# Softmax division behind the product with the values, its reciprocals carried to rows through DRAM

## Chip, core and metric

One core of one Trainium2 chip runs the whole program in one launch. The metric is the device time of that launch in microseconds (us); lower is better. All data are float32; products run on TensorE as fp32r splits (a high and a low part).

## What is computed

A stack of four attention layers (kinds MLA, SWA, FOX, MLA) on a 512 x 1024 sequence, then a second block with four token mixers (two of them attention), a gated feed-forward part and a gated embedding. What the change touches is the softmax that every attention head ends with, here of the dense layers:

```python
def one_block(n):
    s = jnp.einsum('bqhd,bkhd->bhqk', q_blk, k, preferred_element_type=jnp.float32) * scale
    ...
    s = jnp.where(k_pos[None, :] <= q_pos[:, None], s, NEG_INF)
    p = jax.nn.softmax(s, axis=-1).astype(v.dtype)
    return jnp.einsum('bhqk,bkhd->bqhd', p, v)
...
return (o * jax.nn.silu(gate)) @ w_out
```

SWA adds the exponential of a sink to the sum. There are 16 heads in each of the four layers, taken in 8 pairs, and 8 heads (4 pairs) in the mixers: 72 heads, 36 pairs.

## The kernel before

The engines' order is not written by hand. The program is traced in Python, and a scheduler reorders the instructions of each engine by its own estimate of when each could run; each engine, and SP's queue of transfers, then works through its list strictly in that order. So an edit can move instructions that it does not touch.

`pairs` runs a layer's heads. For each pair it prepares the next pair (`prep`: projections of queries and keys on TensorE, splits on ACT and DVE, and in MLA small SBUF moves through SP, L477), then runs `attend` for both heads, joins their outputs into one tile `og` (L462, L463; 64 rows a head, queries along the free axis), computes the gate `u` (`gate`, L606) and multiplies in `gated` (L468 to L470), on POOL for every pair but the layer's last, where DVE does it. The result is split into the high and low operands of the output projection.

`attend` does one head. TensorE makes the scores of four query blocks into PSUM tiles `ps_s`; DVE adds the mask or bias and takes the row maximum (L403); a few 128x4 instructions make the exponent's bias (L409 to L415); ACT takes four exponentials in place in tile `p` and sums each row (L419). Then DVE takes one reciprocal of the four sums (L422) and the four blocks of `p` are scaled by it: on DVE in the layers (L427, four instructions a head), in the mixers two on ACT (L429), one on DVE and one on POOL (L431). TensorE transposes the scaled blocks into `ps_t` (L443), ACT and DVE split them into `pth` and `ptl` (L184, L185), and TensorE multiplies them with the values into the one PSUM tile `ps_o` (L452), which the join empties. PSUM tiles: three `ps_acc`, two `ps_s`, two `ps_t`, one `ps_o`.

```python
nc.vector.reciprocal(st[:, 3], st[:, 2])
for i in range(T):
    a = sc[:, off[i]:off[i] + w[i]]
    how = ("vvvv" if "cq" in s.phase_tags else "aavp")[i]
    if how == "v":
        nc.vector.tensor_scalar_mul(a, a, st[:, 3, i:i + 1])
```

Weights stream in through SP (L135, L146) into six tiles `wr`; ACT rounds each to `wh` (L138) and POOL subtracts for `wl` (L139), which frees `wr` again. In `mixers`, `rel_head` calls `attend` and the joined `og` is split without a gate. FOX has one trip through DRAM already: its forget values are stored (L719, tile `forget`) and read back, one row spread over 128 partitions (L256, tile `rope`).

Of the kernel before, what the change touches and what calls it, by code (L numbers as in the profile page):

```python
# [9 lines left out]
F32 = mybir.dt.float32  # L10
# [11 lines left out]
BUFS = dict(x=4, act=8, wr=6, wh=6, wl=6, st=6)  # L22
# [66 lines left out]
class Kern:  # L89
# [300 lines left out]
    def attend(s, s_mm, k0s, bias, scale, v, sink=None, shift=None):  # L390


        nc = s.nc
# [86 lines left out]
    def mla(s, j, li, xT, g_next):  # L480
# [63 lines left out]
        def head(d, p, e):  # L544
# [7 lines left out]
            return s.attend(s_mm, [0] * T, s.causal, scale, s.vsel(v, e))  # L552
# [33 lines left out]
    def pairs(s, order, prep, head, Wg, g0, xT, oT):  # L586

        order = list(order)
        u = {order[0]: s.gate(order[0], Wg, g0, xT)}
        d = prep(order[0])  # L590
        for p, after in zip(order, order[1:] + [None]):
            og = s.t("f", [P, S], name="og")
            nd = prep(after) if after is not None else None
            for e in range(2):
                s.join(og, e, head(d, p, e))
            if p not in u:
                u[p] = s.gate(p, Wg, g0, xT)
            s.gated(p, og, u[p], oT, after is None)
            d = nd
# [46 lines left out]
    def swa(s, j, li, xT, g_next):  # L646
# [24 lines left out]
        def head(d, p, e):  # L671
            hd = 2 * p + e
            q, (kd, kl), win = d
            return s.attend(lambda out, i, k0: s.qk_mm(out, i, k0, q, e, kd, kl), [0, 0, 1, 2],
                            lambda i: win[:, e, 128:] if i == 0 else win[:, e], 0.125, s.vsel(vt[p // 4], (p % 4) // 2),
                            sink=sinks[:, hd:hd + 1])
# [5 lines left out]
    def fox(s, j, li, xT, g_next):  # L682
# [61 lines left out]
        def head(d, p, e):  # L744
            q, (k, kl), v, bs = d
            return s.attend(lambda out, i, k0: s.qk_mm(out, i, k0, q, e, k[:, e], kl[:, e]), [0] * T,
                            lambda i: bs[e][i], 0.125, s.vsel(v, e), shift=cq[:, :, 2 * p + e])
# [195 lines left out]
    def rel_head(s, qk, v, h, e, og, sel=None):  # L943
# [12 lines left out]
        s.join(og, e, s.attend(lambda out, i, k0: s.qk_mm(out, i, k0, q, e, k[:, e], kl[:, e]), [0] * T, bias, 0.125, s.vsel(v, e)))  # L956

    def mixers(s, hT):
        W = s.I["w_in_2"][0]
# [3 lines left out]
        def heads(d, v, pr, h0, m, sel=None):  # L963
            og = s.t("f", [P, S], name="og")
            for e in range(2):
                s.rel_head(d, v[pr], h0 + 2 * pr + e, e, og, sel)
            s.split(og, mix.h(m + pr), mix.l(m + pr))
# [27 lines left out]
        heads(d1, vd, 1, 0, 4, s.sel)  # L995
# [141 lines left out]
```

## Time and profile before

| what | value |
|---|---|
| median of 3 runs | 1758.17 us (1758.05 to 1764.92) |
| the profiled execution's own time | 1762.84 us |
| its span, first to last instruction | 1761.1 us |
| TensorE (PE) busy | 1684.8 us, 96% |
| PE weight loads (PEld) busy | 1435.2 us, 81% |
| VectorE (DVE) busy | 962.0 us, 55% |
| ScalarE (ACT) busy | 873.8 us, 50% |
| GpSimd (POOL) busy | 854.4 us, 49% |
| TensorE's mean granted clock | 0.979 |

Busy shares are of the span of one profiled execution. A matmul's end is modelled and successive matmuls overlap, so a busy PE is not yet a PE at its peak. "Granted clock" is the share of TensorE's full speed that it was allowed in a stretch: 1.0 is 2.4 GHz, 0.5 is 1.2 GHz. The profile also tells, for each instruction that its engine stood idle for, which instruction released it.

### The profile page before, as it was taken

The page shows a single profiled execution, that of the slowest core. Times are in us where ns is not written, and L with a number is a line of the kernel's source. Part 1 is how long each engine was busy: PE and PEld are TensorE (multiplying, and loading weights), DVE is VectorE, ACT ScalarE, POOL GpSimd, SP SyncE. Part 2 cuts the span into 40 slices and gives each one's busy share as a digit, 9 for nine tenths or more (in the row PEclk, how much of TensorE's full clock was granted, in tenths as well). Part 3 has the DMA queues.
Part 4 walks back from the last instruction along what each step waited for, and adds up shares of the span by engine and source line. Part 5 has one row for each costly group of instructions (what it writes and reads, how often), then busy time and mean ns, then how long its engine had stood idle before and what let it go on. Part 6 is the DMA issues. An engine that isn't in the chain of part 4 may idle for free.

```text
span 1761.1 us, 25691 instructions
## 1 busy us (share of the span) xinstructions
PE 1684.8 (96%) x8818; PEld 1435.2 (81%) x8818; DVE 962.0 (55%) x2223; ACT 873.8 (50%) x2054; POOL 854.4 (49%) x775
## 2 busy tenths in 40 slices
PE   8999999999999999999999998999999999999999
PEld 7888878887788888778888877877778888888877
DVE  4587654677654665766587665599544222210053
ACT  4576543666445655633576642755544333332351
POOL 1644534444255665616644523745644444443571
PEclk9999999999999999999999998999999999999999
DMA  5434534322032333314444523332332333332332
GB/s 169 132 98 114 165 104 124 99 70 87 26 97 81 101 88 93 116 51 127 120 110 103 176 61 74 91 81 64 114 90 83 98 96 96 96 100 80 105 99 72
DMA packets 190339, 173.91 MB, mean 99 GB/s; under 512 B 14280, under 2 KB 154952, under 8 KB 190208
## 3 DMA queue, kind: packets, MB, share of 16 engines
q1 hardware_dynamic: 190208, 172.27, 33.9%
q8 instruction: 70, 1.15, 0.3%
q14 instruction: 61, 0.50, 0.1%
HBM read 150.94 MB, written 6.87 MB: 90 GB/s over the span
## 4 chain that ended last, share of the span: by engine, by line
PE 52%; DVE 9%; ACT 2%; issue 2%; POOL 2%; DMA 1%; SPq 0%; ACTq 0%; POOLq 0%; DVEq 0%
PE ps_acc L157 11%; PE ps_acc L158 11%; PE ps_acc L159 11%; PE ps_s L158 4%; PE ps_s L157 4%; PE ps_s L159 4%; PE ps_o L452 2%; PE ps_t L443 2%; DVE p L427 1%; DVE sel L926 1%; ACT p L419 1%; DVE m L925 1%; DVE p L403 1%; PE ps_s L238 1%; DVE ptl L185 1%
## 5 line engine op out<-in xcount | busy, mean ns | idle before, releaser
L139 POOL TENSOR_TENSOR wl<-wr,wh 128x512 fp32r<-128x512 f32 (+2 forms) x362 | 472.7, 1316 | 421.5 <-ACT wh L138 408.7
L138 ACT CAST wh<-wr 128x512 fp32r<-128x512 f32 (+2 forms) x368 | 223.6, 613 | 364.9 <-PE ps_acc L158 125.1
L157 PE MATMUL ps_acc<-act,wh 128*128 128x512 f32 (+1 forms) x880 | 331.5, 377 | 0.9 <-DVE v L620 0.8
L158 PE MATMUL ps_acc<-act,wh 128*128 128x512 f32 (+1 forms) x880 | 330.2, 375 | 0.3 <-DVE act L185 0.2
L159 PE MATMUL ps_acc<-act,wl 128*128 128x512 f32 (+1 forms) x880 | 330.1, 375 | 0.0
L157 PEld LDWEIGHTS ps_acc<-act,wh 128*128 128x128 f32 x880 | 165.6, 188 | 27.9 <-PE ps_acc L159 1.2
L159 PEld LDWEIGHTS ps_acc<-act,wl 128*128 128x128 f32 x880 | 165.3, 188 | 27.5
L158 PEld LDWEIGHTS ps_acc<-act,wh 128*128 128x128 f32 x880 | 165.4, 188 | 27.0 <-DVE act L185 0.7
L419 ACT ACTIVATE p<-p,st 128x256 f32<-128x256 f32 (+3 forms) x288 | 153.5, 537 | 32.8 <-DVE st L410 17.3
L157 PE MATMUL ps_acc<-wh,act 128*128 128x256 f32 (+3 forms) x384 | 134.5, 350 | 7.7 <-ACT act L469 3.1
L185 DVE TENSOR_TENSOR ptl<-ps_t,pth 128x512 fp32r<-128x512 f32 (+1 forms) x200 | 117.6, 597 | 38.5 <-ACT pth L184 37.7
L184 ACT CAST pth<-ps_t 128x512 fp32r<-128x512 f32 (+1 forms) x200 | 100.3, 516 | 72.5 <-PE ps_t L443 63.0
L443 PE MATMUL ps_t<-c_ident,p 128*128 128x128 f32 x672 | 116.9, 283 | 17.3 <-DVE p L427 12.4
L427 DVE TENSOR_SCALAR p<-p,st 128x256 f32<-128x256 f32 (+3 forms) x264 | 132.1, 559 | 1.8
L159 PE MATMUL ps_acc<-wh,act 128*128 128x256 f32 (+3 forms) x384 | 130.7, 341 | 0.1
L158 PE MATMUL ps_acc<-wl,act 128*128 128x256 f32 (+3 forms) x384 | 130.4, 340 | 0.0
L443 PEld LDWEIGHTS ps_t<-c_ident,p 128*128 128x128 f32 x672 | 82.0, 143 | 33.7 <-DVE p L427 13.2
L452 PE MATMUL ps_o<-pth,v 128*128 128x256 f32 (+3 forms) x288 | 90.1, 318 | 6.3 <-DVE og L463 4.4
L452 PE MATMUL ps_o<-ptl,v 128*128 128x256 f32 (+3 forms) x288 | 88.2, 335 | 4.3 <-DVE ptl L185 4.2
L157 PEld LDWEIGHTS ps_acc<-wh,act 128*128 128x128 f32 x384 | 77.8, 203 | 16.0 <-ACT act L469 3.3
L158 PEld LDWEIGHTS ps_acc<-wl,act 128*128 128x128 f32 x384 | 77.7, 202 | 5.1 <-issue 0.5
L159 PEld LDWEIGHTS ps_acc<-wh,act 128*128 128x128 f32 x384 | 77.1, 201 | 5.5 <-DVE act L185 0.3
(371 smaller groups left out, 3801.3 us busy)
## 6 DMA issues: line engine op xcount, KB each, us to landing
wr<-in_w_gate_up_dram SPq DMA_DIRECT2D x88, 256.0 KB, 2.8
wr<-in_fox_w_in_dram SPq DMA_DIRECT2D x60, 256.0 KB, 3.1
wr<-in_w_in_dram SPq DMA_DIRECT2D x48, 256.0 KB, 2.9
wr<-in_w_down_dram SPq DMA_DIRECT2D x44, 256.0 KB, 2.6
wr<-in_swa_w_in_dram SPq DMA_DIRECT2D x40, 256.0 KB, 2.9
wr<-in_mla_w_in_dram SPq DMA_DIRECT2D x32, 256.0 KB, 3.1
qk<-qk SPq DMA_DIRECT2D x32, 256.0 KB, 3.1
wr<-in_mla_w_out_dram SPq DMA_DIRECT2D x32, 256.0 KB, 3.5
```

The source lines that it names most:

```text
L138: nc.scalar.copy(h, raw)
L139: (nc.vector if dve else nc.gpsimd).tensor_sub(l, raw, h.bitcast(F32))
L157: mm(out, lh, rh, start=first, stop=False)
L158: mm(out, lh, rl, start=False, stop=False)
L159: return mm(out, ll, rh, start=False, stop=last)
L184: s.nc.scalar.copy(hi, src)
L185: s.nc.vector.tensor_sub(lo, src, hi.bitcast(F32))
L238: mm(out, q[:, e, c], kd[:, kk], start=True, stop=False)
L419: nc.scalar.activation(a, a, AF.Exp, bias=st[:, 1, i:i + 1], scale=scale, accum_out=st[:, 2, i:i + 1])
L427: nc.vector.tensor_scalar_mul(a, a, st[:, 3, i:i + 1])
L443: nc.tensor.transpose(ps[:, n:n + P], sc[:, c:c + P], s.ident)
L452: nc.tensor.matmul(o[:, j * P:j * P + m], vj, pp[:, c:c + m], start=first, stop=k == 1 and grp[-1] == max(2, grp[-1]) and j == grp[-1], sk ...
```

## The change

`p` stays unscaled: transposes and the product with the values run on the bare exponentials. The four reciprocals of each head go into a tile of the pair, and the pair's joined output is multiplied by them afterwards, queries along the free axis. For that each head's 512 reciprocals have to stand as a row, the same in 64 partitions. The method `rows` makes them so in one of two ways.

- All pairs but the last of a layer or of the mixers (7 pairs in each of four layers, 3 in the mixers: 31 pairs): the 128x4 reciprocals `rs` are stored to a DRAM tile `rows`, 4 bytes an element, one store a head (L469 of the new kernel), and each head's row is read back into 64 partitions of a tile `rr` (L472). Both are issued by SP.
- The last pair (5 in all): the reciprocal instruction writes each value 64 times (tile `rc`), and four TensorE transposes turn that into rows in a `ps_t` tile.

In the layers DVE multiplies the gate `u` by the rows before the gate is used (L483); in the mixers DVE multiplies `og` itself (L987). The DMA scratch of the launch is cut to 8192 bytes.

```diff
-BUFS = dict(x=4, act=8, wr=6, wh=6, wl=6, st=6)
+BUFS = dict(x=4, act=8, wr=6, wh=6, wl=6, st=6, rc=1, rs=4, rr=2)
...
-        nc.vector.reciprocal(st[:, 3], st[:, 2])
-        for i in range(T):
-            a = sc[:, off[i]:off[i] + w[i]]
-            how = ("vvvv" if "cq" in s.phase_tags else "aavp")[i]
-            if how == "v":
-                nc.vector.tensor_scalar_mul(a, a, st[:, 3, i:i + 1])
-            elif how == "a":
-                nc.scalar.mul(a, a, st[:, 3, i:i + 1])
-            else:
-                nc.gpsimd.tensor_mul(a, a, st[:, 3, i:i + 1].to_broadcast([P, w[i]]))
+        r = st[:, 2]
+        nc.vector.reciprocal(rc, r.unsqueeze(2).to_broadcast([P, T, 64]) if len(rc.shape) == 3 else r)
...
+    def sums(s, last):
+
+        rc = s.t("rc", [P, T, 2, 64]) if last else s.t("rs", [P, 32])[:, :2 * T].rearrange("p (a b) -> p a b", a=2)
+        return rc, [rc[:, :, e] if last else rc[:, e] for e in range(2)]
+
+    def rows(s, rc):
+
+
+        if len(rc.shape) == 3:
+            d = s.dram.tile([2, S], F32, name="rows", tag="rows", bufs=3)
+            for e in range(2):
+                s.nc.sync.dma_start(d[e].rearrange("(i p) -> p i", p=P), rc[:, e])
+            r = s.t("rr", [P, S])
+            for e in range(2):
+                s.nc.sync.dma_start(r[64 * e:64 * e + 64],
+                                    bass.AP(tensor=d.tensor, offset=d.offset + e * S, ap=[[0, 64], [1, S]]))
+            return r
+        ps = s.p("t")
+        for i in range(T):
+            s.nc.tensor.transpose(ps[:, i * P:(i + 1) * P], rc[:, i].rearrange("p a b -> p (a b)"), s.ident)
+        return ps
+
-    def gated(s, p, og, u, oT, last):
+    def gated(s, p, og, u, rc, oT, last):
         nc = s.nc
         e = nc.vector if last else nc.gpsimd
+        nc.vector.tensor_mul(u, u, s.rows(rc))
         e.tensor_mul(og, og, u)
...
+            nc.vector.tensor_mul(og, og, s.rows(rc))
             s.split(og, mix.h(m + pr), mix.l(m + pr))
...
-    nc = bacc.Bacc("TRN2", target_bir_lowering=False, num_devices=1)
+    nc = bacc.Bacc("TRN2", target_bir_lowering=False, num_devices=1, dynamic_dma_scratch_size=8192)
```

Since the scheduler orders anew, instructions move on every engine. Three places follow. **DVE, first head of the first layer's seventh pair**, from its last small instruction to the scaling; `p_2296` and `st_2297` are that head's exponentials and statistics. Before:

```order
L412 TENSOR_SCALAR st_2297<-st_2297 128x4
L422 RECIPROCAL st_2297<-st_2297 128x4
L403 ISA p_2363,st_2364<-ps_s_2365,c_mask_814 128x512
L403 ISA st_2364 128x1
L427 TENSOR_SCALAR p_2296<-p_2296,st_2297 128x128
L427 TENSOR_SCALAR p_2296<-p_2296,st_2297 128x256
L427 TENSOR_SCALAR p_2296<-p_2296,st_2297 128x384
L427 TENSOR_SCALAR p_2296<-p_2296,st_2297 128x512
L185 TENSOR_TENSOR ptl_2214<-ps_t_2210,pth_2213 128x256
```

The same head in the changed kernel, where its tiles are `p_2297` and `st_2298`, and `rs_2296` takes the reciprocals:

```order
L413 TENSOR_SCALAR st_2298<-st_2298 128x4
L424 RECIPROCAL rs_2296<-st_2298 128x4
L456 TENSOR_TENSOR og_1993<-ps_o_2115,og_1993 64x512
L623 SCALAR_TENSOR_TENSOR f_2251<-f_2251,ps_acc_2214 128x512
L404 ISA p_2360,st_2361<-ps_s_2362,c_mask_815 128x512
L404 ISA st_2361 128x1
L185 TENSOR_TENSOR ptl_2196<-ps_t_2190,pth_2195 128x512
L404 ISA p_2360,st_2361<-ps_s_2367,c_mask_815 128x384
L404 ISA st_2361 128x1
L483 TENSOR_TENSOR f_2251<-f_2251,rr_2257 128x512
```

The four scalings are gone; the reciprocal has no reader on DVE, and the multiplication of a gate by the rows of an earlier pair stands further on.

**PE, first pair of the first layer**, where the first head's blocks are transposed (`p_808` before, `p_809` now; products of `qk_727` are the second head's scores, of `ckv` and `act` other projections). Before:

```order
L157 MATMUL ps_s_884<-qk_727,qk_651 128x128
L158 MATMUL ps_s_884<-qk_727,qk_651 128x128
L159 MATMUL ps_s_884<-qk_727,qk_651 128x128
L443 MATMUL ps_t_842<-c_ident_63,p_808 128x128 x2
L443 MATMUL ps_t_853<-c_ident_63,p_808 128x128
```

Now:

```order
L436 MATMUL ps_t_839<-c_ident_63,p_809 128x128
L157 MATMUL ps_acc_1027<-ckv_147,wh_967 128x512
L158 MATMUL ps_acc_1027<-ckv_148,wh_967 128x512
L159 MATMUL ps_acc_1027<-ckv_147,wl_968 128x512
L157 MATMUL ps_acc_1027<-ckv_147,wh_975 128x512
L158 MATMUL ps_acc_1027<-ckv_148,wh_975 128x512
L159 MATMUL ps_acc_1027<-ckv_147,wl_976 128x512
L436 MATMUL ps_t_839<-c_ident_63,p_809 128x128
L436 MATMUL ps_t_850<-c_ident_63,p_809 128x128
L157 MATMUL ps_s_890<-qk_727,qk_651 128x256
L158 MATMUL ps_s_890<-qk_727,qk_651 128x256
L159 MATMUL ps_s_890<-qk_727,qk_651 128x256
```

Before, the transposes stood behind all scores of the second head; now the first three stand ahead of its scores of 256 columns.

**SP's queue, first pair of the first layer**: moves of queries and keys (`qk`), weight loads (`wr`). Before:

```order
L477 DMA qk<-qk 64x1024
L477 DMA qk<-qr 32x1024
L146 DMA wr<-in_mla_w_kv_up_dram 128x512
L477 DMA qk<-qr 32x1024
L146 DMA wr<-in_mla_w_kv_up_dram 128x512
L135 DMA wr<-in_mla_w_in_dram 128x4x128 x2
```

Now:

```order
L469 DMA rows<-rs 128x4x1
L472 DMA rr<-rows 64x512
L493 DMA qk<-qk 64x1024
L493 DMA qk<-qr 32x1024 x2
L146 DMA wr<-in_mla_w_kv_up_dram 128x512
L469 DMA rows<-rs 128x4x1
L146 DMA wr<-in_mla_w_kv_up_dram 128x512
L472 DMA rr<-rows 64x512
```

A store and a read-back for each head stand among the moves and weight loads, with a weight load between the second head's two.

## Rows read from the trace of the kernel before

**Rows 1.** Page, part 1: busy us, share of the span, instructions.

```profile
PE 1684.8 (96%) x8818; PEld 1435.2 (81%) x8818; DVE 962.0 (55%) x2223; ACT 873.8 (50%) x2054; POOL 854.4 (49%) x775
```

**Rows 2.** Windows, six attention stretches: PE, PEld, DVE, ACT, POOL busy, clock, DMA.

```profile
84.00:241.00 157.00, 150.48 (x817) 128.22 (x816) 113.20 (x307) 100.62 (x269) 69.96 (x65) 0.98 0.44 121
331.00:468.00 137.00, 126.83 (x674) 106.52 (x673) 107.39 (x301) 88.47 (x238) 53.35 (x41) 0.95 0.23 70
564.00:769.00 205.00, 202.30 (x1125) 174.85 (x1124) 133.06 (x329) 128.19 (x308) 118.36 (x116) 0.99 0.33 95
879.00:1033.00 154.00, 149.63 (x819) 127.48 (x818) 112.62 (x306) 99.99 (x269) 68.93 (x63) 0.99 0.44 122
1168.00:1213.00 45.00, 40.15 (x215) 33.01 (x213) 44.77 (x127) 22.97 (x58) 18.43 (x19) 0.89 0.23 59
1255.00:1296.00 41.00, 36.70 (x176) 29.74 (x176) 25.73 (x53) 23.23 (x57) 18.42 (x17) 0.92 0.30 93
sum 739.00, PE 706.09 PEld 599.82 DVE 536.77 ACT 463.46 POOL 347.45; mean PE 117.68 PEld 99.97 DVE 89.46 ACT 77.24 POOL 57.91
```

**Rows 3.** Waits of PE: total us, times, longest.

```profile
PE ps_t L443 <- DVE p L427: 12.4, 17, 2.5
...
PE ps_s L238 <- DVE st L403: 5.5, 7, 1.6
...
PE ps_t L443 <- DVE ptl L185: 4.5, 6, 2.4
PE ps_o L452 <- DVE og L463: 4.4, 10, 0.9
```

**Rows 4.** Chain that ended last, share of the span by line.

```profile
by line: PE ps_acc L157 11.0%; PE ps_acc L158 10.7%; PE ps_acc L159 10.6%; PE ps_s L158 3.6%; PE ps_s L157 3.6%; PE ps_s L159 3.6%; PE ps_o L452 2.2%; issue 2.0%; PE ps_t L443 1.9%; DVE p L427 1.1%; DVE sel L926 1.0%; ACT p L419 0.9%; DVE m
```

**Rows 5.** Timeline 203 to 209 us, ACT, DVE, PE: start, us, instruction, idle before.

```profile
203.77 0.19 ACT L419 ACTIVATION_READ_ACCUMULATOR p<-p,st 128x1 f32 x1
...
203.99 0.18 DVE L422 RECIPROCAL st<-st 128x4 f32<-128x4 f32 x1 [6.65 <-ACT p L419]
204.67 3.87 DVE L427 TENSOR_SCALAR p<-p,st 128x128 f32<-128x128 f32 x4
...
207.69 0.50 PE L443 MATMUL ps_t<-c_ident,p 128*128 128x128 f32 x2 [2.52 <-DVE p L427]
```

**Rows 6.** Windows around that wait and behind the last such; columns as in rows 2.

```profile
205.00:209.40 4.40, 1.88 (x13) 1.37 (x12) 4.40 (x8) 0.64 (x2) 2.46 (x3) 1.00 0.32 114
209.40:212.80 3.40, 3.40 (x13) 2.92 (x12) 3.16 (x8) 2.40 (x5) 1.21 (x1) 0.50 0.69 221
...
1001.30:1004.70 3.40, 3.40 (x13) 3.01 (x14) 2.84 (x9) 2.80 (x5) 0.54 (x1) 0.50 0.59 192
```

**Rows 7.** Groups by line: count, busy us, mean ns, idle before.

```profile
L427 DVE TENSOR_SCALAR p<-p,st 128x256 f32<-128x256 f32 (+3 forms) x264 | 132.1, 559 | 1.8
L443 PE MATMUL ps_t<-c_ident,p 128*128 128x128 f32 x672 | 116.9, 283 | 17.3 <-DVE p L427 12.4 <-DVE ptl L185 4.5
```

**Rows 8.** Tile og: duration ns min, median, max.

```profile
L468 DVE TENSOR_TENSOR og<-og,f x4: 691/692/927, 250.8 to 1042.4; 128x512 f32<-128x512 f32 x4
```

**Rows 9.** Window of the feed-forward part, PE never idle; columns as in rows 2.

```profile
1400.00:1440.00 40.00, 40.00 (x178) 33.13 (x177) 9.03 (x11) 13.29 (x23) 19.16 (x15) 1.00 0.33 95
```

**Rows 10.** DMA issues: count, KB each, median us to landing.

```profile
qk<-kr SPq DMA_DIRECT2D x32, 128.0 KB, 2.6
...
ckv<-in_ln_b_dram SPq DMA_DIRECT2D x4, 512.0 KB, 8.5
...
forget<-f SPq DMA_DIRECT2D x1, 32.0 KB, 1.6
cw<-in_conv_w_dram SPq DMA_DIRECT2D x2, 1.5 KB, 2.1
...
f<-in_rel_bias_dram SPq DMA_DIRECT2D x1, 1.0 KB, 4.3
```

**Rows 11.** Waits of SP's queue: total us, times, longest.

```profile
SPq L135 <- POOL wl L139: 755.1, 309, 19.7
```

More of the change, by code (lines that the diff above doesn't have):

```diff
@@ L387, in stage_end, with attend @@
         return nxt
-    def attend(s, s_mm, k0s, bias, scale, v, sink=None, shift=None):
+    def attend(s, s_mm, k0s, bias, scale, v, rc, sink=None, shift=None):
         nc = s.nc
@@ L542, in prep, with head @@
             return qt, kt, vt[pr]
-        def head(d, p, e):
+        def head(d, p, e, rc):
             qt, kt, v = d
@@ L550, in s_mm @@
                 return s.mm3(out, qh[:96, c], ql[:96, c], kh[:96, kk], kl[:96, kk], True, True)
-            return s.attend(s_mm, [0] * T, s.causal, scale, s.vsel(v, e))
+            return s.attend(s_mm, [0] * T, s.causal, scale, s.vsel(v, e), rc)
         s.pairs(range(8), prep, head, Win, 672, xT, oT)
@@ L593, in pairs @@
             nd = prep(after) if after is not None else None
+            rc, rcs = s.sums(after is None)
             for e in range(2):
-                s.join(og, e, head(d, p, e))
+                s.join(og, e, head(d, p, e, rcs[e]))
             if p not in u:
                 u[p] = s.gate(p, Wg, g0, xT)
-            s.gated(p, og, u[p], oT, after is None)
+            s.gated(p, og, u[p], rc, oT, after is None)
             d = nd
@@ L669, in prep, with head @@
             return qt, [k[:, pr // 2] for k in K[kp]], win
-        def head(d, p, e):
+        def head(d, p, e, rc):
             hd = 2 * p + e
@@ L674, in head @@
             return s.attend(lambda out, i, k0: s.qk_mm(out, i, k0, q, e, kd, kl), [0, 0, 1, 2],
-                            lambda i: win[:, e, 128:] if i == 0 else win[:, e], 0.125, s.vsel(vt[p // 4], (p % 4) // 2),
+                            lambda i: win[:, e, 128:] if i == 0 else win[:, e], 0.125, s.vsel(vt[p // 4], (p % 4) // 2), rc,
                             sink=sinks[:, hd:hd + 1])
@@ L742, in prep, with head @@
             return qt, kt, V[g][pr], bs
-        def head(d, p, e):
+        def head(d, p, e, rc):
             q, (k, kl), v, bs = d
             return s.attend(lambda out, i, k0: s.qk_mm(out, i, k0, q, e, k[:, e], kl[:, e]), [0] * T,
-                            lambda i: bs[e][i], 0.125, s.vsel(v, e), shift=cq[:, :, 2 * p + e])
+                            lambda i: bs[e][i], 0.125, s.vsel(v, e), rc, shift=cq[:, :, 2 * p + e])
         s.pairs([6, 7, 0, 1, 2, 3, 4, 5], prep, head, Win, 3088, xT, oT)
@@ L941, in rel_values, with rel_head @@
         return vt
-    def rel_head(s, qk, v, h, e, og, sel=None):
+    def rel_head(s, qk, v, h, e, og, rc, sel=None):
         nc = s.nc
@@ L954, in rel_head @@
             bias = lambda i: bb[:, off[i]:off[i] + (i + 1) * P] if i else b[:, 384:]
-        s.join(og, e, s.attend(lambda out, i, k0: s.qk_mm(out, i, k0, q, e, k[:, e], kl[:, e]), [0] * T, bias, 0.125, s.vsel(v, e)))
+        s.join(og, e, s.attend(lambda out, i, k0: s.qk_mm(out, i, k0, q, e, k[:, e], kl[:, e]), [0] * T, bias, 0.125, s.vsel(v, e),
+                             rc))
     def mixers(s, hT):
+        nc = s.nc
         W = s.I["w_in_2"][0]
@@ L961, in mixers, with heads @@
         vm = s.rel_values(W, 2888, hT)
-        def heads(d, v, pr, h0, m, sel=None):
+        def heads(d, v, pr, h0, m, sel=None, last=False):
             og = s.t("f", [P, S], name="og")
+            rc, rcs = s.sums(last)
             for e in range(2):
-                s.rel_head(d, v[pr], h0 + 2 * pr + e, e, og, sel)
+                s.rel_head(d, v[pr], h0 + 2 * pr + e, e, og, rcs[e], sel)
+            nc.vector.tensor_mul(og, og, s.rows(rc))
             s.split(og, mix.h(m + pr), mix.l(m + pr))
@@ L994, in mixers @@
         s.conv(W, hT, mix, 1)
-        heads(d1, vd, 1, 0, 4, s.sel)
+        heads(d1, vd, 1, 0, 4, s.sel, True)
         return s.stage_end(s.I["w_out_2"][0], mix, s.I["g_mix_post_2"][0], s.I["g_ffn_pre_2"][0])
```

## Prediction

> **What bounds the kernel now.** I read the busy shares first: PE is busy for 96% of the span [rows 1], so only its idle time and its low clock can be won. The windows of the six stretches in which `attend` runs say how much lies there: of 739 us PE is busy for 706.1, so 32.9 us are idle, and the granted clock is below 1.0 in each [rows 2]. With two levels, 1.0 and 0.5, a mean of 0.95 over 137 us means 13.7 us at the half level; the six stretches together give 6.3 + 13.7 + 4.1 + 3.1 + 9.9 + 6.6 = 43.7 us at 1.2 GHz, which cost PE at most half of that, 21.8 us. The ceiling for anything that only unblocks attention is therefore 54.7 us. Next, who PE waits for: the largest single entry is the transpose waiting for DVE's scaling, 12.4 us in 17 waits [rows 3]. The chain that ended last puts a little more there: L427 holds 1.1% of the span, 19.4 us [rows 4]. One such wait, read in order of time, shows the mechanism: ACT had the last sum at 203.96, the reciprocal ended at 204.17, the four scalings took until 208.54, and PE's transposes started at 207.69 after 2.52 us of standing [rows 5]. The 3.4 us behind that stretch were granted 0.50, after a stretch in which PE was busy for 1.88 of 4.40 us [rows 6].
>
> **What goes.** 264 scalings leave DVE, 132.1 us of its time [rows 7], and with them the step between exponentials and transposes: four instructions of 559 ns, 2.2 us a head. Three gains on PE's path follow.
> (a) The waits for the scaling themselves: between 12.4 us (rows 3) and 19.4 us (the chain). I take 19.4, since the chain also counts scalings that delayed PE through something else.
> (b) The half clock behind them. Five low stretches of 3.4 us in the traced span start within 1.7 us of such a wait; [rows 6] show the second and the fifth. Five times 3.4 at half rate lose at most 8.5 us; I take 7.
> (c) DVE's other lateness. PE also waits for score reductions (5.5), for splits (4.5) and for the joins that free the one `ps_o` (4.4), 14.4 us in all [rows 3]. DVE is busy for 536.8 of 739 us in these stretches [rows 2]; without the scalings, and with the new work below, it is some 105 us less, a fifth. I take a third of the 14.4, 5 us; bounds 0 and 14.4.
> In the mixers the sixteen scalings on ACT and eight on POOL go too; neither engine ends a wait of PE in [rows 3], so I cost them at nothing.
>
> **What is given back.** (d) The scheduler packs the shorter head more tightly. Counting in the two orders the PE work between a head's last score product and its first transpose, at 225 ns for 512 columns (178 of them in 40 us of unbroken work [rows 9]), the mean over 72 heads falls from 8.5 to 7.4 us. So 1.1 us of cover go where the latency loses 2.4 us (the scalings and a 176 ns reciprocal): nearly half of (a), 9 us, comes back as waits for the exponentials. It could be nothing, or all of (a) where a head was moved by more, as the first pair's transposes were.
>
> **What is added.** (e) Twenty transposes for the last pairs. A transpose holds PE for 116.9 / 672 = 0.174 us [rows 7]: 3.5 us. They need only sums, so they are in time for a multiplication that waits for the last join anyway.
> (f) DVE's multiplications, 36 of 512 columns; the nearest row is the same shape at 0.69 us [rows 8], 25 us in all. In the layers they act on the gate and so stand beside the head's own work; in the mixers they stand between join and split, and behind the last pair PE waits for that: 0.7 us.
> (g) The trip through DRAM, 31 times. DVE's multiplication stands in order, so a late trip stops every score reduction and split queued behind it on DVE, and PE after them. No row of before stores 4-byte elements to DRAM. The nearest: a store of whole rows lands in 1.6 us, loads in 4-byte elements in 2.1 us (384 of them) and 4.3 us (256), a 128 KB load in 2.6 us [rows 10]. The read-back moves 128 KB, so the trip takes 1.6 + 2.6 = 4.2 us at the least and 4.3 + 2.6 = 6.9 at the upper small row; I take 2.1 + 2.6 = 4.7, since that row is the nearest in number of elements. What covers it is the work that the order puts between the pair's second reciprocal and its multiplication, the larger of DVE's and PE's. Priced with the same 225 ns for 512 columns, 21 of 31 pairs have 8 us or more there; the short ones are 3.9, 4.0, 4.3, 4.3, 4.7, 5.5, 5.6, 6.2, 6.3 and 6.9 us. At 4.7 us DVE stands for 0.8 + 0.7 + 0.4 + 0.4 = 2.3 us in all; at 6.9 for 17.3. I put 2.3 on the path.
> SP itself: 62 stores and 62 reads join its queue, and each read waits there for its store to land, which holds back the weight loads and `qk` moves behind it by 1.6 to 4.3 us. SP already stands 755.1 us waiting for POOL to free a weight tile [rows 11], six loads ahead of use, and none of PE's waits in [rows 3] or in the chain names a weight tile, so I cost this at nothing. If that cover is gone, PE waits by the same 1.6 to 4.3 us each time.
> The smaller DMA scratch costs nothing that I can see: every issue in [rows 10] is SP's own.
>
> The page *DMA: Bandwidth & Descriptors* of the Trainium skill, section Rules for kernel authors, speaks against this trip: it says that a non-contiguous last dimension becomes one descriptor an element, and that transposing by a rearranged access pattern is 19 times slower than the hardware's DMA transpose. Estimated from that figure and the 1.6 us store, a store would take 30 us and the kernel would lose hundreds of us. The loads in 4-byte elements of [rows 10] do not bear such a ratio out at this size; no run here shows a store of that kind.
>
> **The sum.** -19.4 - 7 - 5 + 9 + 3.5 + 0.7 + 2.3 = -15.9 us. Against the profiled execution's own 1762.8 us that gives 1746.9; its time stands 4.7 us above the median of the runs, so against the median I predict 1742 us, 0.9% faster.
>
> **The rivals.**
> *The latency was the only cover lost* (same): the tighter order gives all of (a) and (b) back, and PE waits for ACT's exponentials instead of DVE's scalings. For it: the first pair's transposes now stand ahead of the second head's scores. Against: in [rows 5] ACT was done 3.7 us before PE started, more than any tightening seen on average. It leaves -5 + 3.5 + 0.7 + 2.3 = +1.5, so 1757 to 1760.
> *The whole stretch loosens* (faster still): DVE's relief reaches most of the 54.7 us ceiling, because each avoided stand also keeps the clock up. For it: the stretch at 1168 us, where DVE is busy for 44.8 of 45 us and the clock is 0.89 [rows 2]. Against: that stretch has few scalings on DVE. Four fifths of the ceiling, 44 us, less the 6.5 us of (e) to (g), give -37, about 1721.
> *The trip lands late* (slower): place, DVE's multiplication by `rr`; price, the sum over pairs of trip less cover. At 7.0 us DVE's standing eats all that (a) to (f) win; at 7.9 it is 27 us and the kernel is slower by half a percent; at 9 it is 41 us, near 1781. For it: a load behind other transfers lands in 8.5 us [rows 10], stores of single elements are in no row, and the changed queue puts a weight load, which may itself wait for a free tile, between the store and the read of the very first pair, whose cover is 4.3 us. Against: the two small 4-byte loads and the forget store, all under 4.5.
>
> **How the numbers follow.** A change within 0.5%, 8.8 us, can't be told from none here. Forecast 0.55 (1728 to 1753 by the bounds of (a), (c), (d) and (g); about a tenth of that lies within 0.5%), the given-back case 0.2, the loosened stretch 0.1, the late trip 0.15. So faster 0.59, same 0.26, slower 0.15. The range 1718 to 1766 holds the forecast, the given-back case, most of the loosened one, and leaves out most of the late trip.
>
> **What would show it.** Right: no scaling rows; PE's wait before the transposes smaller than 12.4 us and naming ACT's exponentials; DVE's busy time near 855 us; stores to `rows` landing in about 2 us; DVE's idle before L483 on `rr` a few us in all; a mean clock above 0.979. Wrong: DVE standing for `rr` by tens of us, PE waits for splits and reductions growing with it, SP's weight loads named among PE's waits, or the transposes waiting for ACT as long as they waited for DVE.

## The result, and the profile after

The changed kernel takes **2095.57 us** (2092.9 to 2099.65, 4 runs) against 1759.38 us (1758.05 to 1764.92, 4 runs) for the kernel before: ratio 1.1901, 95% interval 1.1875 to 1.1928. It is slower by a fifth, and far outside the predicted range.

Busy time first. Page of the changed kernel, part 1 (busy us, share of the span, instructions), to be set beside [rows 1]:

```profile
PE 1754.1 (84%) x8838; PEld 1488.7 (71%) x8838; DVE 862.0 (41%) x1995; ACT 869.5 (42%) x2038; POOL 836.8 (40%) x767
```

DVE lost 100 us net as planned, the scalings less the multiplications by the rows, and no computing engine got new work to speak of. Yet the span grew from 1761.1 to 2091.1 us. PE's idle time went from 76.3 to 337.0 us, 260.7 us more, and its busy time grew by 69.3 us, although twenty transposes are all that it was given: the granted clock fell from 0.979 to 0.910. Behind the stand of 11.78 us that is shown below, for example, the window from 440.4 to 443.8 us was granted 0.50, which is 1.2 GHz. So this is a kernel that waits, and the questions are where and for what.

Where: the same five stages in both kernels, cut at the first statistics of the normalization behind each of the four attention layers (columns as in [rows 2]). Before:

```profile
0.00:256.40 256.40, 237.54 (x1288) 204.62 (x1289) 160.31 (x415) 148.48 (x396) 117.41 (x121) 0.97 0.47 134
256.40:482.40 226.00, 215.22 (x1174) 182.77 (x1173) 149.78 (x388) 124.88 (x307) 87.94 (x67) 0.97 0.26 79
482.40:788.30 305.90, 296.11 (x1667) 257.51 (x1666) 181.82 (x431) 168.46 (x389) 166.43 (x165) 0.98 0.32 90
788.30:1047.20 258.90, 249.85 (x1373) 215.31 (x1372) 171.94 (x431) 143.35 (x389) 127.65 (x126) 0.99 0.42 118
1047.20:1761.10 713.90, 686.10 (x3322) 574.95 (x3321) 298.11 (x564) 288.61 (x573) 355.01 (x296) 0.98 0.30 89
```

After:

```profile
0.00:341.30 341.30, 255.27 (x1293) 218.99 (x1294) 140.82 (x360) 149.47 (x396) 116.11 (x121) 0.87 0.41 106
341.30:642.20 300.90, 229.32 (x1181) 193.93 (x1180) 124.88 (x333) 124.29 (x307) 87.37 (x67) 0.86 0.27 66
642.20:1014.90 372.70, 313.27 (x1663) 268.82 (x1662) 155.14 (x374) 169.18 (x389) 163.90 (x165) 0.89 0.30 79
1014.90:1370.20 355.30, 273.82 (x1382) 234.92 (x1381) 150.22 (x375) 143.82 (x389) 126.33 (x126) 0.86 0.38 92
1370.20:2091.10 720.90, 682.43 (x3326) 571.99 (x3324) 290.90 (x560) 282.72 (x557) 343.05 (x288) 0.98 0.31 89
```

Each of the four layers, with seven trips through DRAM, lost 67 to 96 us; the rest of the program, with three trips in over 700 us, lost 7. The loss goes where the trips are.

For what: waits of all engines in the changed kernel (total us, times, longest),

```profile
DVE f L483 <- DMA rr<-rows: 183.1, 16, 18.8
...
DVE f L483 <- issue: 86.0, 8, 14.1
```

of PE,

```profile
PE ps_o L445 <- DVE ptl L185: 80.0, 14, 11.8
PE ps_s L157 <- DMA qk<-kr: 34.7, 9, 8.2
PE ps_t L436 <- DVE ptl L185: 33.2, 4, 15.3
```

and of SP's queue:

```profile
SPq L135 <- POOL wl L139: 562.9, 247, 17.1
SPq L472 <- DMA rows<-rs: 517.7, 62, 11.2
```

DVE stands before the multiplication by `rr` in 24 of 28 pairs, 269.1 us in all (the second line is the same wait, where the profile has no landing to name). PE waits for splits, which stand behind that multiplication on DVE, and for the moves of `kr`, which have nothing to do with it. SP stands 517.7 us before the read-backs; its wait for POOL, the cushion of [rows 11], is down from 755.1 to 562.9. The issues of the same kernel (count, KB each, median us to landing), to be set beside [rows 10], say why:

```profile
qk<-qk SPq DMA_DIRECT2D x32, 256.0 KB, 5.7
...
rr<-rows SPq DMA_DIRECT2D x62, 128.0 KB, 4.5
...
rows<-rs SPq DMA_DIRECT2D x62, 2.0 KB, 8.9
```

A store of 2 KB takes **8.9 us** to land (7.3 to 11.4, where the trace tells the landing, for 42 of the 62), where I had put 2.1. One trip in the second layer shows how that becomes a stand of PE. SP's timeline (start, us, instruction):

```profile
412.12 0.37 SPq L469 DMA_DIRECT2D rows<-rs  x1
421.03 0.48 SPq L472 DMA_DIRECT2D rr<-rows  x1
...
423.25 0.46 SPq L469 DMA_DIRECT2D rows<-rs  x1
434.02 0.47 SPq L472 DMA_DIRECT2D rr<-rows  x1
```

DVE's and PE's timelines behind it (in brackets the idle time before, and what ended it):

```profile
419.36 0.18 DVE L424 RECIPROCAL rs<-st 128x4 f32<-128x4 f32 x1
...
423.01 0.69 DVE L185 TENSOR_TENSOR ptl<-ps_t,pth 128x512 fp32r<-128x512 f32 x1
439.24 0.69 DVE L483 TENSOR_TENSOR f<-f,rr 128x512 f32<-128x512 f32 x1 [15.54 <-DMA rr<-rows]
439.85 0.55 DVE L185 TENSOR_TENSOR ptl<-ps_t,pth 128x384 fp32r<-128x384 f32 x1
```

```profile
440.46 0.58 PE L445 MATMUL ps_o<-ptl,v 128*128 128x256 f32 x1 [11.78 <-DVE ptl L185]
```

The second head's reciprocals were ready at 419.5, but SP stood from 412.5 to 421.0 for the first head's store, and issued the second store only at 423.25. That landed at 434.0, its read-back 5.2 us later. DVE had stood since 423.7, the split of `ptl` stood behind it, and PE stood for 11.78 us for that split. From the second reciprocal, where the prediction's trip starts, to the multiplication that is 19.7 us and not 4.7; from the first head's store it is 27.

### The profile page after: what moved, and what is told of

The parts are those of the page before. It is cut to its first block, busy times and chain, and to the rows that moved or that the text cites. A ratio compares the mean times of both kernels' runs of the same rounds, so it can differ in the third digit from the quotient of the medians.

```text
span 2091.1 us, 25698 instructions
## 1 busy us (share of the span) xinstructions
PE 1754.1 (84%) x8838; PEld 1488.7 (71%) x8838; DVE 862.0 (41%) x1995; ACT 869.5 (42%) x2038; POOL 836.8 (40%) x767
## 2 busy tenths in 40 slices
DMA packets 228035, 182.18 MB, mean 87 GB/s; under 512 B 48008, under 2 KB 188680, under 8 KB 227904
## 3 DMA queue, kind: packets, MB, share of 16 engines
HBM read 159.06 MB, written 7.00 MB: 79 GB/s over the span
## 5 line engine op out<-in xcount | busy, mean ns | idle before, releaser
L159 PE MATMUL ps_acc<-act,wl 128*128 128x512 f32 (+1 forms) x880 | 339.7, 386 | 7.4 <-POOL wl L139 7.4
L157 PE MATMUL ps_acc<-act,wh 128*128 128x512 f32 (+1 forms) x880 | 341.8, 389 | 1.6 <-DVE qk L204 1.1
L158 PE MATMUL ps_acc<-act,wh 128*128 128x512 f32 (+1 forms) x880 | 339.1, 385 | 0.3 <-DVE act L185 0.2
L157 PEld LDWEIGHTS ps_acc<-act,wh 128*128 128x128 f32 x880 | 171.4, 195 | 30.2 <-issue 2.3
L158 PEld LDWEIGHTS ps_acc<-act,wh 128*128 128x128 f32 x880 | 171.0, 194 | 27.8 <-DVE act L185 0.7
L436 PE MATMUL ps_t<-c_ident,p 128*128 128x128 f32 x672 | 132.9, 304 | 66.2 <-DVE ptl L185 33.2
L445 PE MATMUL ps_o<-ptl,v 128*128 128x256 f32 (+3 forms) x288 | 94.6, 357 | 80.1 <-DVE ptl L185 80.0
L436 PEld LDWEIGHTS ps_t<-c_ident,p 128*128 128x128 f32 x672 | 90.7, 155 | 82.1 <-ACT p L420 38.1
L483 DVE TENSOR_TENSOR f<-f,rr 128x512 f32<-128x512 f32 x28 | 21.3, 762 | 269.1 <-DMA rr<-rows 183.1
L445 PEld LDWEIGHTS ps_o<-ptl,v 128*128 128x128 f32 x288 | 61.2, 212 | 89.3 <-DVE ptl L185 85.3
L484 POOL TENSOR_TENSOR og<-og,f 128x512 f32<-128x512 f32 x28 | 36.1, 1288 | 149.0 <-DVE og L456 149.0
L404 DVE CUSTOM_DVE_ANT_0 p<-ps_s,c_mask 128x512 f32<-128x512 f32 (+3 forms) x128 | 59.9, 483 | 74.4 <-PE ps_t L436 42.9
```

The lines of the kernel that those rows point to most:

```text
L157: mm(out, lh, rh, start=first, stop=False)
L158: mm(out, lh, rl, start=False, stop=False)
L159: return mm(out, ll, rh, start=False, stop=last)
L404: nc.vector.tensor_tensor_reduce(out=sc[:, off[i]:off[i] + w[i]], in0=ps[:, c:c + w[i]], in1=bias(i), op0=ALU.add, op1=ALU.max, scale=1.0, ...
L436: nc.tensor.transpose(ps[:, n:n + P], sc[:, c:c + P], s.ident)
L445: nc.tensor.matmul(o[:, j * P:j * P + m], vj, pp[:, c:c + m], start=first, stop=k == 1 and grp[-1] == max(2, grp[-1]) and j == grp[-1], sk ...
```

## The experiments

All are edits to the changed kernel unless said otherwise; times are medians of runs, ratios against the kernel before on the same chip (1758.9 to 1762.1 us).

**Without DRAM.** All 36 pairs take TensorE's way, four transposes a pair, with two `rc` tiles instead of one:

```diff
-            rc, rcs = s.sums(after is None)
+            rc, rcs = s.sums(True)
...
-            rc, rcs = s.sums(last)
+            rc, rcs = s.sums(True)
```

> All 36 pairs bring their reciprocals into rows by four TensorE transposes; no trip through DRAM. Theory A (the late trip: stores landing in 8.9 us, DVE's multiplication and SP's queue standing for them) expects the loss to vanish: 144 transposes at 0.11 to 0.17 us are 16 to 24 us of PE, less the 16 that my sum gave to the removed scalings, so 1745 to 1775 us. Theory C (the tighter order alone makes PE stand) expects most of the loss to stay: above 1950 us. Theory B (the 4-byte stores hold up the other transfers in the DMA engines) expects the same as A here.

1766.23 us, 1.0027 (1.0011 to 1.0044). The whole loss is in the way through DRAM. The division behind the product is no gain in this form either: each reciprocal that writes its value 64 times holds DVE for 1752 ns.

**The trip made free.** No stores; the read-backs fetch a row of ones from a constant:

```diff
-            d = s.dram.tile([2, S], F32, name="rows", tag="rows", bufs=3)
-            for e in range(2):
-                s.nc.sync.dma_start(d[e].rearrange("(i p) -> p i", p=P), rc[:, e])
...
-                                    bass.AP(tensor=d.tensor, offset=d.offset + e * S, ap=[[0, 64], [1, S]]))
+                                    bass.AP(tensor=s.C["c_tri"].tensor, offset=s.C["c_tri"].offset, ap=[[0, 64], [1, S]]))
```

> The stores are left out and the read-back takes a row of ones from a constant, so the output lacks the division in 31 pairs. SP still issues 62 reads, DVE still multiplies. Theory A and B expect 1735 to 1755 us: what the removed scalings are worth with a trip that costs nothing. Theory C expects above 1950 us.

1734.98 us, 0.9853 (0.9837 to 0.987). This is what taking the scalings out is worth, 26 us, with the transposes of the last pairs and DVE's multiplications paid.

**The stores back, with nobody waiting.** As the last, but with the 4-byte stores. From the changed kernel, only the read-back differs:

```diff
-                                    bass.AP(tensor=d.tensor, offset=d.offset + e * S, ap=[[0, 64], [1, S]]))
+                                    bass.AP(tensor=s.C["c_tri"].tensor, offset=s.C["c_tri"].offset, ap=[[0, 64], [1, S]]))
```

> The 62 stores in 4-byte runs stay, but nobody reads them: the read-back takes a row of ones from a constant and waits for no store (output without the division in 31 pairs). Theory A expects the time of the run without stores, within 15 us, since nothing waits for a landing. Theory B expects the loss to stay: 1900 us or more, with weight loads and moves of queries landing as late as in the changed kernel (5.5 us and 5.7 us for 3.5 and 3.1 before).

1841.9 us, 1.0462 (1.0438 to 1.0485): 107 us more, for 62 stores of 2 KB whose data no instruction and no transfer reads. Theory A, within 15 us of the run without stores, is out; theory B's mechanism is there, but not its 1900 us. SP's and PE's waits in the run without stores, and then part 1 of its page:

```profile
SPq L490 <- DMA qk<-qk: 61.9, 32, 4.4
...
PE ps_t L436 <- ACT p L420: 2.2, 9, 0.4
PE ps_s L157 <- DMA qk<-kr: 2.3, 2, 1.3
```

```profile
PE 1665.2 (96%) x8838; PEld 1423.7 (82%) x8838; DVE 869.2 (50%) x1995; ACT 868.6 (50%) x2038; POOL 841.8 (49%) x767
```

and the same two with them:

```profile
SPq L493 <- DMA qk<-qk: 135.5, 32, 11.6
...
PE ps_t L436 <- ACT p L420: 31.7, 16, 8.4
PE ps_s L157 <- DMA qk<-kr: 24.8, 8, 6.7
```

```profile
PE 1697.6 (92%) x8838; PEld 1445.1 (79%) x8838; DVE 862.7 (47%) x1995; ACT 868.1 (47%) x2038; POOL 839.4 (46%) x767
```

The moves of `qk` behind a store are late (the longest wait for one goes from 4.4 to 11.6 us) and PE waits for them; in all its idle time grows by 75 us (span less busy), and its busy time by another 32 at a clock that falls from 0.990 to 0.964. But only the two MLA layers have such moves. Cut at the same places as above, they lost 62 of the 107 us; FOX lost 23, SWA 9 and the rest 14. In FOX it is the forget rows spread over the partitions that come late: POOL's wait for them, 17.6 us without stores, is 45.0 with them.

```profile
POOL b L754 <- DMA rope<-forget: 45.0, 7, 10.8
```

In the trace of the changed kernel 16 transfers with a recorded landing were issued by SP while a store was still on its way; none of them landed before that store did. That order is nothing special to a slow store: in the run below with the elements 64 bytes apart it holds for 51 of 51 transfers too. What differs is how long the store takes.

**The stores on another queue.** As the last, with the stores issued by ACT:

```diff
-                s.nc.sync.dma_start(d[e].rearrange("(i p) -> p i", p=P), rc[:, e])
+                s.nc.scalar.dma_start(d[e].rearrange("(i p) -> p i", p=P), rc[:, e])
```

> As the run with unread stores, but ACT's queue issues the stores in place of SP's (output without the division in 31 pairs). If a store holds up the landing of what is issued behind it on the same queue only, the 107 us above the run without stores go and the time is 1735 to 1765 us. If it holds up every transfer on the same DMA engines, whichever queue issued it, the time stays at 1800 us or more.

1852.59 us, 1.0524 (1.0483 to 1.0566). The stores now have a hardware queue of their own, and PE still waits 34.2 us for `kr` moves on SP's queue. The hold-up is not one of SP's order. Part 3 of the page (queue, packets, MB, and the time that the packets took as a share of 16 engines' span) says whose packets take longer, first SP's queue and then ACT's:

```profile
q1 hardware_dynamic: 195168, 180.40, 40.5%
q10 hardware_dynamic: 32736, 0.13, 1.0%
```

The stores' own packets take 1.0% of the span. The packets of SP's queue, as many as in the run without stores, take 40.5% of 1853.0 us where they took 36.6% of 1729.2. So it is the packets of the other transfers that take longer.

**The whole trip, its result unused.** Stores, waits of SP and read-backs as in the change, but DVE multiplies by something else, in the mixers likewise:

```diff
-        nc.vector.tensor_mul(u, u, s.rows(rc))
+        r = s.rows(rc)
+        nc.vector.tensor_mul(u, u, r if last else u)
```

> The whole trip stays, each read-back waiting in SP's queue for its store to land, but no instruction reads the rows (in 31 pairs DVE multiplies the gate, in the mixers the output, by itself, so the output lacks the division). It takes DVE's standing away and leaves SP's. If SP's waiting costs as much as DVE's, about half of the 254 us between the run with unread stores and the changed kernel stays: 1950 to 1990 us. If DVE's standing is all, it equals the run with unread stores, 1842 us. If SP's queue is what counts, it stays above 2050 us.

2015.87 us, 1.1452 (1.1402 to 1.1502): 174 us above the run with stores alone, of the 254 us that the text had to divide, which is none of its three cases. SP and PE there:

```profile
SPq L472 <- DMA rows<-rs: 522.4, 62, 11.5
...
PE ps_s L157 <- DMA qk<-kr: 89.3, 10, 18.4
```

With SP standing for each store, the moves behind it start late as well as land late. What DVE's own standing for `rr` adds is the 80 us from here to 2095.57.

**The same bytes in longer runs.** The DRAM row is laid out partition by partition, so a store is 128 runs of 16 bytes instead of 512 of 4, and DVE reads `rr` with a stride:

```diff
-                s.nc.sync.dma_start(d[e].rearrange("(i p) -> p i", p=P), rc[:, e])
+                s.nc.sync.dma_start(d[e].rearrange("(p i) -> p i", i=T), rc[:, e])
...
-            return r
+            return r.rearrange("d (p i) -> d i p", i=T)
```

> The same trip, but the DRAM row is laid out partition by partition, so a store has 128 runs of 16 bytes in place of 512 runs of 4, and DVE reads the row back with a stride of four. If the landing follows the number of runs, a store lands in 2.2 to 4 us and the read-back in 2.6 to 4.5; the trip of 5 to 8 us is mostly covered: 1740 to 1820 us. If the landing is a fixed cost of such stores, it stays near 8 us and the time near 2050 us.

1754.55 us, 0.9964 (0.9949 to 0.9978): 341 us gone by the layout alone. Its issues:

```profile
rr<-rows SPq DMA_DIRECT2D x62, 128.0 KB, 3.5
...
rows<-rs SPq DMA_DIRECT2D x62, 2.0 KB, 1.9
```

DVE still stands 19.8 us for `rr`, in 9 pairs, and SP 85.9 us before the read-backs; the strided multiplication takes 1084 ns instead of 693.

**Half way.** The same with 256 runs of 8 bytes, and the matching stride in DVE's reads:

```diff
-                s.nc.sync.dma_start(d[e].rearrange("(p i) -> p i", i=T), rc[:, e])
+                s.nc.sync.dma_start(d[e].rearrange("(a p i) -> p a i", p=P, i=2), rc[:, e].rearrange("p (a i) -> p a i", i=2))
```

> Edit to the run with 16-byte runs: the DRAM row is laid out in runs of 8 bytes, 256 in a store instead of 128, and DVE reads rr with a stride of two elements instead of four; everything is divided. Theory (the landing goes with the number of runs in a store, beyond some fixed part): with 1.9 us at 128 runs and 8.9 at 512, a straight line gives 4.2 us at 256, and the time stands between 1755 and 2096 in the way that a trip longer by 2.3 us brings: waits of DVE for rr and of SP for the stores some tens of us more, 1770 to 1850 us. Rival 1 (what is slow is an element of 4 bytes as such): 256 runs of 8 bytes land in about 2 us like the 16-byte ones, and the time is within 10 us of 1755. Rival 2 (any store below 16 bytes a run is as slow as the 4-byte one): 8 to 9 us to landing, near 2000 us or more.

1798.21 us, 1.0208 (1.0176 to 1.0239). The store lands in 4.0 us, as the straight line said:

```profile
rows<-rs SPq DMA_DIRECT2D x62, 2.0 KB, 4.0
```

**One store a pair.** The run with unread stores, with only the first head's (and, in a second run, `(1,)` in place of `range(1)`: only the second head's):

```diff
-            for e in range(2):
+            for e in range(1):
                 s.nc.sync.dma_start(d[e].rearrange("(i p) -> p i", p=P), rc[:, e])
```

> Edit to the run with the 4-byte stores that nobody reads: only the first head's store of each pair is left, 31 stores instead of 62; all else is as there, and as there 31 pairs are not divided by their sums. Theory (each 4-byte store by itself holds up what is in flight behind it): half the stores, half the loss, so half of 107 us, 1735 + 54 = about 1789 us, between 1770 and 1805. Rival 1 (the loss comes where the two stores of a pair, or a store and the next weight load, stand in one another's way, so a single store a pair is nearly free): within 12 us of the 1735 without any store. Rival 2 (something that comes with the first store of a pair sets the loss, such as the second operand that waits in any case): over 1815. SP's wait for the moves of qk, 61.9 us without stores and 135.5 with 62, should come to about 95 by the theory.

1756.21 us, 0.9965 (0.995 to 0.998): 21 of the 107 us, not half, though SP waits 100.0 us for the moves of `qk`, near the 95 of the text. The second head's alone:

> Edit to the run with the 4-byte stores that nobody reads: only the second head's store of each pair is left, 31 of 62; 31 pairs are not divided by their sums, as there. Theory (place decides: the second head's store stands ahead of the next pair's moves of qk, so it is what made 86 of the 107 us): about 1735 + 86 = 1821 us, at least 1800. Rival (the two stores of a pair make it together: either alone is covered by the slack that the moves have, and only the sum of both hold-ups is over it): 1745 to 1765, like the run with the first head's store alone (1756).

1790.24 us, 1.0166 (1.0128 to 1.0204): 55 us. Neither text had this right. Which store it is counts, but not by standing ahead of the moves of `qk`: of the 12 pairs in the MLA layers that have such a move to come, SP issues it directly behind the first head's store in 10, and directly behind the second's, which is the dearer, in 7. SP's wait for these moves does not tell the two apart either (100.0 and 93.4 us). What makes the second dearer stays open. The two together cost some 30 us more than the sum of each alone.

**Half the elements.** Both stores, each with two of four query blocks:

```diff
-                s.nc.sync.dma_start(d[e].rearrange("(i p) -> p i", p=P), rc[:, e])
+                s.nc.sync.dma_start(d[e, :256].rearrange("(i p) -> p i", p=P), rc[:, e, :2])
```

> Edit to the run with the 4-byte stores that nobody reads: both stores stay, each with two of its four query blocks, 256 elements of 4 bytes instead of 512; 31 pairs are not divided by their sums, as there. Theory (what a store holds up goes with its number of elements, and the slack of the transfers behind it covers a hold-up of some 4 us): landings near 4 us as with 256 runs of 8 bytes, and a time of 1740 to 1765 us. Rival 1 (a store of 4-byte elements is slow whatever their number): like the 1842 with all elements, over 1815. Rival 2 (the loss goes with the number of elements in a straight line): 1735 + 54, about 1789.

1826.21 us, 1.0363 (1.0323 to 1.0403), my first rival. 256 elements land no sooner than 512 (by the 15 landings of 62 that the trace tells), while 256 runs of 8 bytes take 4.0:

```profile
rows<-rs SPq DMA_DIRECT2D x62, 1.0 KB, 9.4
```

So the landing does not go with the number of elements in the store, and two explanations were left: a 4-byte element is slow as such, or writes side by side in DRAM wait for one another.

**Elements apart.** Stores as in the run with unread stores, the same 512 elements of 4 bytes, but every 64 bytes in DRAM (and in a second run every 512, with 128 in place of 16):

```diff
-            d = s.dram.tile([2, S], F32, name="rows", tag="rows", bufs=3)
+            d = s.dram.tile([2, S, 16], F32, name="rows", tag="rows", bufs=3)
...
-                s.nc.sync.dma_start(d[e].rearrange("(i p) -> p i", p=P), rc[:, e])
+                s.nc.sync.dma_start(d[e, :, 0].rearrange("(i p) -> p i", p=P), rc[:, e])
```

> Edit to the run with the 4-byte stores that nobody reads: the 512 elements of a store go to DRAM 64 bytes apart instead of side by side; 31 pairs are not divided by their sums, as there. Theory (separate writes into the same stretch of DRAM wait for one another, some 60 to 70 ns a write, and a stretch of 512 bytes takes 128 of them in the dense layout): at 64 bytes apart a stretch of 512 bytes takes 8, so landings of 1.5 to 3 us and a time near that without stores, 1735 to 1755 us. Rival 1 (a 4-byte element is slow as such): landings of about 9 us and 1815 to 1845 us as with the dense layout. Rival 2 (scattered writes cost more, since each touches DRAM by itself): over 1850.

> As the run with elements 64 bytes apart, but 512 bytes apart, 256 KB of DRAM for a head's row; 31 pairs are not divided by their sums. Theory (writes into the same stretch wait for one another): no two elements share a stretch of 512 bytes, 1735 to 1755 us, the same as at 64 bytes apart if the stretch is 64 bytes or less. Rival 1 (a 4-byte element is slow as such): 1815 to 1845 us. Rival 2 (scatter costs more): over 1850, and more than at 64 bytes apart.

1733.95 us, 0.9854 (0.9837 to 0.987), and 1734.0 us, 0.9852 (0.9834 to 0.987): the time without any store. The issues at 64 bytes apart, and at 512:

```profile
rows<-rs SPq DMA_DIRECT2D x62, 2.0 KB, 2.3
```

```profile
rows<-rs SPq DMA_DIRECT2D x62, 2.0 KB, 2.1
```

This settles what makes the store slow: neither the element size nor the number of packets (228035 in the whole run, as with the dense layout), but that the elements lie side by side.

**Towards a better kernel.** First the rows made on chip: one transpose of both heads' reciprocals to 8x128, a copy by ACT, and one store of 512-byte runs a pair:

```diff
-            for e in range(2):
-                s.nc.sync.dma_start(d[e].rearrange("(i p) -> p i", p=P), rc[:, e])
+            ps = s.p("t")
+            s.nc.tensor.transpose(ps[:2 * T, :P], rc.rearrange("p a b -> p (a b)"), s.ident)
+            c = s.t("rw", [2 * T, P])
+            s.nc.scalar.copy(c, ps[:2 * T, :P])
+            s.nc.sync.dma_start(d.rearrange("a (b p) -> (a b) p", p=P), c)
```

> One TensorE transpose turns the pair's 128x8 reciprocals into eight rows of 128, ACT copies them out of PSUM and one store of eight 512-byte runs takes them to DRAM; the read-back is as in the change, so DVE reads without a stride. Half the stores, no small runs. If runs are what made the stores land late, a store lands in about 1.6 us and nothing is held up behind it; DVE's multiplication takes 0.69 us for 1.08 in the run with 16-byte runs: 1740 to 1755 us. If the added step and the ps_t tile cost more than that, 1755 to 1775 us.

1781.44 us, 1.0118 (1.0081 to 1.0156), a miss. Two more steps stand in the queues of PE and ACT before the trip can start: SP waits 52.9 us for ACT's copies, 16.5 the longest. And DVE waits in all 28 pairs:

```profile
DVE f L486 <- DMA rr<-rows: 64.4, 28, 4.8
```

Then the run with 16-byte runs, with the first pair of the MLA layers and of FOX on TensorE, where the cover was short:

```diff
-            rc, rcs = s.sums(after is None)
+            rc, rcs = s.sums(after is None or (p == order[0] and g0 != 1536))
```

> The run with 16-byte runs, but the first pair of the two MLA layers and of FOX also goes over TensorE: in that run DVE stood 4.9, 4.9 and 2.3 us for the rows there. If these waits are on PE's path, they go against twelve transposes (2 us): 1744 to 1752 us. If they are covered, 1754 to 1758 us.

**1748.28 us, 0.9931 (0.9907 to 0.9955)**: the fastest median of those that divide every pair, 0.7% below the kernel before. With more pairs there (the second of those layers, all of SWA):

```diff
-            rc, rcs = s.sums(after is None or (p == order[0] and g0 != 1536))
+            rc, rcs = s.sums(after is None or p in order[:2] or g0 == 1536)
```

> Edit to the run with 16-byte runs and the first pair of three layers on TensorE: now also the second pair of those layers, and all eight pairs of SWA, go through TensorE's transposes; 14 pairs in the layers are left for DRAM. In that run DVE still stood for rr before five of SWA's pairs (1.0, 1.5, 1.6, 2.4 and 0.2 us) and one of the first FOX pairs (1.0). Theory (a pair belongs on TensorE where its cover is shorter than the trip, and only there): removes those 8 us of standing, of which little reached PE, and adds four transposes for ten more pairs, 7 us of PE: between 1745 and 1755, no better than the 1748 before it. Rival (each trip also costs through SP, whose moves and weights wait behind the reads, so fewer trips are better as long as TensorE's transposes are late nowhere): SP's waits for rows fall from 74.7 to about 35, and the time to 1738 to 1744.

1752.15 us, 0.9945 (0.9922 to 0.9968): nothing more, as the intervals overlap. DVE's standing for `rr`, 7.8 us in the run before, is down to 1.6, but it now stands 5.6 us for rows that TensorE transposes, and PE's wait for ACT's exponentials goes from 5.3 to 10.0 us.

## Why the prediction was wrong

**(a) to (f), the removal: right in kind, too small.** They gave -18.2 us; the run with a free trip shows -26 by the medians, and -32 between the two profiled executions, to which the next numbers belong. PE's wait before the transposes names ACT's exponentials, as forecast, but is 2.2 us and not the 9 that (d) gave back. The size that was off is (b): PE's busy time fell from 1684.8 to 1665.2 us with twenty transposes added, and the clock rose from 0.979 to 0.990. By the two levels that is some 39 us less at 1.2 GHz, worth about 19 us, where I had allowed five stretches and 8.5 us at most. (Of those five the trace has four within 1.7 us of a wait for a scaling; two more start 2.5 and 2.7 us behind one.) Idle time fell by 12.3 us, less than the 15.4 that (a), (c) and (d) made together. (e) alone was not measured; the 31 further pairs on TensorE cost 31 us against the free trip, about 1.0 us a pair with their long reciprocals, beside my 0.7. (f)'s 0.69 us is the median that was measured.

**(g), the trip: the step that failed.** I took a store of 2.1 us and put 4.3 as its upper end; it takes 8.9. The row I called nearest, a load of 384 elements of 4 bytes, was near in number and wrong in direction: small reads from DRAM are no price for small writes side by side. The read-back, 2.6 in the sum, took 4.5. And I added store and read once a pair, but SP issues in order, so the second head's trip starts behind the first one's, as the 19.7 us above show. The range did not hold all that the terms allowed: with (a), (c), (d) and (g) at their bounds the sum runs from 1722 to 1773 us, where I wrote 1728 to 1753. The measured time is far outside of both.

**"I cost this at nothing" (SP): failed too, and dearer.** The step argued from weight tiles, whose loads run six ahead of use. What stands behind the store in SP's queue in the MLA layers and has no such lead are the moves of `qk`, which PE waits for (34.7 us in the changed kernel, 89.3 in the run whose `rr` is unused), and I had named them in the same sentence. The "1.6 to 4.3 us each time" was the right form at half the price or less: SP's 62 waits come to 8.4 us each.

**What no step had:** that a store nobody waits for delays transfers issued behind it. That is 107 us of the loss, SP's standing 174, DVE's standing 80; against them the gain of 26. These four are the steps from one run to the next, so they add up to the 336 by themselves, and the shares hold for this order of putting the parts back.

**The rivals.** "The trip lands late" named the right place, DVE's multiplication by `rr`, and a chance of 0.15; its price at a trip of 9 us, 1781, counted DVE's standing alone, which is the smallest of the three, and the store alone took 8.9. The other two rivals speak of cover and relief, and the free trip answers them: the relief was real, 26 of the 37 us that the second gave.

**The rule that I set aside.** By the trace, the dense store costs 8.9 us where a store of whole rows takes 1.6 [rows 10], a ratio of 5.6. The Trainium skill, page *DMA: Bandwidth & Descriptors*, section Rules for kernel authors, warned against this access pattern, with 19 times: the direction and the "hundreds of us" of my estimate from it agree. That factor of the Trainium skill is against the hardware's DMA transpose, which no run here has, so the ratio of 5.6 does not test it. Another rule of that section of the Trainium skill, one descriptor an element, does not explain the time: the same elements at 64 bytes apart, in as many packets, land in 2.3 us. The section Specifications of that page of the Trainium skill says that a transfer below 512 bytes is done as a read, a change and a write. This would fit writes that wait for their neighbours, but the elements apart are as small and are not slow, and no run here shows the reads: the 159.06 MB that the changed kernel reads from DRAM are 8.1 more than before, which are the 62 read-backs.

## What to carry to other kernels

Price a small store by its layout at the far end as well as by its bytes: elements of a few bytes from many partitions that interleave in DRAM landed four to nearly five times later than the same elements apart or in 16-byte runs. An order of a transfer on a queue has three costs, each to be asked for by itself: who waits for its data, what the issuing queue holds back while it waits, and which transfers in flight land later because of it. Where the nearest row differs in direction from what is to be priced, its value is no upper end, and a forecast built on it needs a wider range.

## What was unexpected of the hardware

- **Small writes side by side in DRAM are slow.** Dense 4-byte elements land in 8.9 us (512 of them) and 9.4 (256), dense runs of 8 bytes in 4.0, of 16 bytes in 1.9; elements 64 or 512 bytes apart in 2.3 and 2.1. In 512 bytes of DRAM that is 128, 64 and 32 writes, and the landing about doubles with each step; at 8 writes and at one it stays near 2 us. So the 60 to 70 ns a write of my text (8.9 us over 128, 4.0 over 64, 1.9 over 32) hold for the dense layouts alone. That such writes wait for one another is the reading that fits, and is not shown. How large the stretch is that they would share stays open: it was seen only that 64 bytes apart is enough. Nor was the number of writes in a stretch told apart from the number of transfer engines that write into it, since the layout changes both.
- **Such a store holds up what is in flight behind it**, from SP's queue and from ACT's alike (1842 and 1853 us against 1735 without stores). On a queue of their own the stores' packets took 1.0% of the span, and the packets of the others took longer. What in the transfer engines makes it so was not tried.
- **The loss is not additive**: first head's store alone 21 us, second's alone 55, both 107. That each alone is partly covered by slack which both together use up is only argued.
